# Halving the mixer lane's rate and holding its work behind the main line in a hybrid decoder trunk

## The chip, the cores and the metric

The kernel runs on one core of one Trainium2 chip. The metric is the device time of one execution in microseconds; lower is better. The engines are named as the profile names them: PE is TensorE, DVE is VectorE, ACT is ScalarE, POOL is GpSimd, SP is the queue that issues the loads and stores.

## The reference, cut to what matters

The kernel computes DEPTH = 2 layers over 1024 tokens of width 1024. Each layer is a mixer of three head groups, a channel MLP and a gated embedding:

```python
def hybrid_layer(h, p_i, ...):
    xn = rmsnorm(h, attn_norm_g)
    z = xn @ w_in
    za, zq, zk, zv, zc = jnp.split(z, ...)
    ya = chunk_gmlp(za, ...)
    q = apply_rope(rmsnorm(q, q_norm_g), cos, sin)
    k = apply_rope(rmsnorm(k, k_norm_g), cos, sin)
    yb = swa_sink_attention(q, k, v, sinks)          # window 128
    yc = s5_ssm(zc, ...)
    y = jnp.concatenate([rmsnorm(ya, ...), rmsnorm(yb, ...), rmsnorm(yc, ...)], axis=-1)
    h = h + y @ w_out
    hn = rmsnorm(h, mlp_norm_g)
    h = h + jnp.square(jax.nn.relu(hn @ w_ff1)) @ w_ff2      # D_FF = 4096
    gate = jax.nn.sigmoid(rmsnorm(h, ple_norm_g) @ w_ple_gate)
    return h + gate * (p_i @ w_ple_proj)
```

## The kernel before

**Halves and windows.** The tokens are cut into two halves of 512 (h = 0, 1). The dense part of a layer for one half (the MLP and the gate) is a *window*; there are four, in the order (layer 0, half 0), (0, 1), (1, 0), (1, 1), called windows 0 to 3 here. A window goes through the MLP in 8 chunks: four groups of 24 matmuls (FF1, 128x512 each, with a high and a low part of each operand), then eight groups of 12 (FF2), which add into H. Behind the last chunk comes the *tail*: the sum of squares of H, its rstd, and then the gate with eight groups of 24. That makes 1728 matmuls of the main line in a window.

**The lane.** The mixer of the window after the next one (projection, attention, S5, gMLP, then mix_out with eight groups of 24 matmuls by w_out) is a Python generator, a *lane*. The window's code yields every 12 matmuls, and at each such step `tick` advances the lane by RATE pieces. So the program text itself alternates main line and lane. After that the tile framework's scheduler places the instructions of each engine by its own model of time, and may move a lane instruction ahead of main ones that were traced before it. Each engine then runs its instructions strictly in the resulting order. The left lane (the mixer of half 1 of layer 0) runs at RATEL = 3.0, and is `nxt` for window 0.

**The norm's scale.** `rstd_wide` (from L283) sums over the partitions by one matmul into a PSUM bank, tag "o", which exists once and is shared by every caller with that tag; then VectorE scales it (L289), makes a seed (L293) and goes three rounds (ACT's square L295, VectorE L296 and L297), reading the bank until the last L296. mix_out calls it for the MLP's norm (its output is `rbc`, read by r at L1344), the window's tail for the gate's norm (read by gt at L1390).

**Banks.** Of the eight PSUM banks mm and s have two each, x, p, t and o one. In the MLP `fbank` goes round mm, mm, x; in the gate round mm, s, x, mm, s, p, so the sixth group behind one writes its bank again, which gt of that group (L1390) must have read.

**Weights.** `load_w` loads a 512 KB piece, ACT casts its high part (L104), VectorE subtracts for the low part (L105). The main line's ring has three w buffers, the mixer's has two.

**Around the change.** The first window follows mix_out(0, 0), which `run` drives by itself (`finish`), with the left lane advancing beside it; the left lane's attention prepares k (L1078 to L1117: gt, tab, kt, k, kst), transposes it on PE (pk L1120, kT L1122), and prepares and transposes q (rt, qst L1143 to L1151, pq L1188, qt L1191), then multiplies (pss L1201).

Of the kernel before, what the change touches and what calls it, by code (L numbers as in the profile page):

```python
# [16 lines left out]
P = 128  # L17
# [4 lines left out]
NK = D // P  # L22
# [16 lines left out]
PASSES = ((0, 0), (1, 0), (0, 1))  # L39


RATE, RATE0, RATEL = 3.0, 2.0, 3.0


class Ring:

    def __init__(self, trunk, stg, pool, plan, ahead):
        self.t, self.stg, self.pool, self.plan, self.ahead = trunk, stg, pool, plan, ahead
        self.loaded = []
# [13 lines left out]
class Trunk:  # L63


    def __init__(self, tc, ctx, a):
        self.tc, self.ctx, self.a = tc, ctx, a
        self.nc = nc = tc.nc
        self.V, self.S, self.G, self.T, self.Q = nc.vector, nc.scalar, nc.gpsimd, nc.tensor, nc.sync
        self.lanes, self.nbank, self.nz, self.flags = [], 0, 0, set()  # L70
        self.X, self.R, self.H, self.hst = {}, {}, {}, {}

    def pool(self, stack, name, bufs=1, **kw):
        return stack.enter_context(self.tc.tile_pool(name=name, bufs=bufs, **kw))
# [123 lines left out]
    def finish(self, e):  # L198
        self.until(lambda: e[3])

    def main(self, gen):
        for _ in gen:
            self.tick()

    def wait(self, *flags):
        while not all(f in self.flags for f in flags):
# [1116 lines left out]
    def window(self, l, h, stages):  # L1323

        a, V, S, G, T, Q = self.a, self.V, self.S, self.G, self.T, self.Q
        st, fp = self.stage("ff", h)
        F, H = self.fring, self.H[h]
        last = l == DEPTH - 1
        A = fp.tile([P, 2, 4, HALF], F32R, name="A")
        nch = DFF // 512  # L1330

        def f2(w, m, ps, tail):
            V.tensor_tensor(H[:, m], H[:, m], ps, ALU.add)  # L1333
            if tail is not None:
                self.add_sq(H, m, tail, fp, "r", 2)
                self.split_x(h, m, self.g_ple(l, m))

        for c in range(nch):
            tail = None
            for m in range(4):  # L1340
                w, ps = F.next(), self.fbank()
                self.main(self.cm(ps, w, 0, self.X[h], range(NK)))
                r = fp.tile([P, 512], F32, tag="r", name="r", bufs=2)
                V.scalar_tensor_tensor(r, ps, 0.0, self.R[h][1], ALU.max, ALU.mult)  # L1344
                q = fp.tile([P, 512], F32, tag="r", name="q", bufs=2)
                S.activation(A[:, 0, m], r, AF.Square)  # L1346
                S.activation(q, r, AF.Square)  # L1347
                V.tensor_tensor(A[:, 1, m], q, A.bitcast(F32)[:, 0, m], ALU.subtract)  # L1348
            if c == nch - 1:
                self.until(lambda: stages <= self.flags and ("prep", 1) in self.flags)  # L1350
                pst, pp = self.stage("ple", h)
                pjs = []

                def load_pj():
                    if len(pjs) < NK:
                        t = pp.tile([P, 512], F32, tag="pj", name="pj", bufs=4)
                        Q.dma_start(t, self.pj[l][h][len(pjs)])
                        pjs.append(t)

                for _ in range(4):  # L1360
                    load_pj()
                tail = fp.tile([P, 512], F32, name="nacc")
                self.new_x(h)
            for i in range(4):
                w = F.next()
                if i == 0:

                    pss = [self.fbank() for _ in range(2)]
                    for j in range(2):
                        self.main(self.cm(pss[j], w, j * P, A, (0, 1, 2), stop=False))  # L1370
                    for j in range(2):
                        self.main(self.cm(pss[j], w, j * P, A, (3,), start=False))
                    self.tick()
                    self.tick()
                    for j in range(2):
                        f2(w, j, pss[j], tail)
                    continue
                for j in range(2):
                    ps = self.fbank()
                    self.main(self.cm(ps, w, j * P, A, range(4)))  # L1380
                    f2(w, 2 * i + j, ps, tail)
        self.rstd_wide(tail, D, EPS, h, (fp, "r", 2))
        acc = None
        if not last:
            acc = fp.tile([P, 512], F32, name="nacc")
        for m in range(NK):
            pg = self.fbank(("mm", "s", "x", "mm", "s", "p"))
            self.main(self.cm(pg, F.next(), 0, self.X[h], range(NK)))
            t = fp.tile([P, 512], F32, tag="r", name="gt", bufs=2)
            V.tensor_tensor(t, pg, self.R[h][1], ALU.mult)  # L1390
            S.activation(t, t, AF.Tanh, scale=0.5)
            V.scalar_tensor_tensor(t, t, 1.0, pjs[m], ALU.add, ALU.mult)
            load_pj()
            V.scalar_tensor_tensor(H[:, m], t, 0.5, H[:, m], ALU.mult, ALU.add)
            if not last:
                self.add_sq(H, m, acc, fp, "r", 2)
            else:
                po = self.ps.tile([P, 4, P], F32, tag="to"[m % 2], name="po")
                for b in range(4):
                    T.transpose(po[:, b], H[:, m, b * P:(b + 1) * P], self.ident)  # L1400
                ot = pp.tile([P, 4, P], F32, name="ot", bufs=4)
                S.copy(ot, po)  # L1402
                Q.dma_start(a["out"][0, h * HALF:(h + 1) * HALF, m * P:(m + 1) * P].rearrange("(b p) c -> p b c", p=P),
                            ot)
        if not last:
            Q.dma_start(self.hs[h], H)
            nl = self.lane(self.rstd_lane(acc, D, EPS, h))
            self.step(nl)
            self.new_x(h)
            for k in range(NK):  # L1410
                self.split_x(h, k, self.g_attn(l + 1, k))
        pst.close()
        st.close()
        self.hst[h].close()
        if not last:
            self.finish(nl)
            self.flags.add(("x", l + 1, h))
# [61 lines left out]
    def run(self):  # L1479
        self.setup()  # L1480
        zws, self.zw = ExitStack(), None
        self.zw = self.pool(zws, "zw", 4, side=self.side(0), reuse_waits="tile")
        xs, xp = self.stage("xin", 0)
        left = self.lane(self.left_lane(), RATEL)
        for _ in self.first_x(0, xp, left):
            pass
        x1 = self.lane(self.first_x(1, xp))
        gen = self.project0()
        z0 = self.lane(gen)
        self.until(lambda: x1[3] and ("zq", 0, 0) in self.flags)  # L1490
        xs.close()
        self.until(lambda: {"zg", "rotary"} <= self.flags)
        zws.close()
        self.lanes.remove(z0)
        pzs = ExitStack()
        self.zpools.append(self.pool(pzs, "pz", 2, side=self.side(0), reuse_waits="tile"))
        self.lane(self.gmlp(0, 0, 0, "x", [("attn", 0, 0)]), RATE0)
        self.until(lambda: True)
        self.lane(self.attention(0, 0, 0), RATE0)
        self.main(gen)  # L1500
        self.main(self.embed())
        self.until(lambda: {("attn", 0, 0), ("gm", 0, 0)} <= self.flags)
        self.zpools.pop()
        pzs.close()
        self.finish(self.lane(self.mix_out(0, 0, self.fring, "mm", 3)))
        seq = [(l, h) for l in range(DEPTH) for h in range(2)]
        nxt = left
        for i, (l, h) in enumerate(seq):
            self.window(l, h, self.stages(*seq[i + 1]) if i + 1 < len(seq) else set())
            if i + 1 < len(seq):  # L1510
                self.finish(nxt)
            if i + 2 < len(seq):
                nxt = self.lane(self.mix_lane(*seq[i + 2]), RATE)
# [30 lines left out]
```

## Time and profile before

| | us |
|---|---|
| median of 3 runs (lowest, highest) | 2381.81 (2376.33, 2382.33) |
| the profiled execution, its own time | 2379.47 |
| its span in the trace | 2377.7 |
| PE busy | 2321.7 |
| VectorE busy | 1552.6 |
| ScalarE busy | 1026.9 |

The span is what the trace covers; the execution's own time is 1.8 us longer. PE's busy time is modelled from pipelined matmuls, so a busy share of 98% says that PE seldom waits, not that it runs at its peak. Window 0 begins at about 337 us; the last gt of the gates of windows 0 to 2 starts at 842.36, 1411.99 and 1969.14 us. A timeline row names start, busy time, engine, line and operation, and in square brackets the idle time just before it with what ended it.

### The profile page before, as it was taken

The numbers are of one execution on the slowest core, as the hardware profiler recorded it, in microseconds if no ns is written. First come the engines' busy times: TensorE is split into PE (matmuls) and PEld (weight loads), VectorE is DVE, ScalarE is ACT, GpSimd is POOL, SyncE is SP. The second block draws the span as 40 slices with busy tenths as digits, with TensorE's granted clock in tenths as the row PEclk, the third lists the DMA queues.
The fourth block names the chain that finished last, engine by engine and source line by source line (L and its number), as shares of the span: only waits on it lengthen the run. The fifth ranks groups of instructions, "written<-read, shape, count | busy, mean of one in ns | idle before, by whom it ended". The sixth has DMA issues, their size and how long they took to land. (4 is left out here: it accounts for less than half of the span.)

```text
span 2377.7 us, 29270 instructions
## 1 busy us (share of the span) xinstructions
PE 2321.7 (98%) x10941; PEld 1884.9 (79%) x10941; DVE 1552.6 (65%) x2700; ACT 1026.9 (43%) x1787; POOL 5.4 (0%) x15
## 2 busy tenths in 40 slices
PE   7998899999999999999999999999999999999998
PEld 5887677788788887777888888777888888888887
DVE  7877768675966765675585774676657675444455
ACT  7427646433334443553342543464334443322333
POOL 0000000000000000000000000000000000000000
PEclk9997999999999999999999999999999999999999
DMA  8663632253553335324443344422434425333333
GB/s 244 191 203 120 210 100 61 79 179 101 145 156 99 114 126 146 103 75 139 128 135 120 102 138 132 137 76 80 159 103 141 127 80 150 98 95 94 96 94 101
DMA packets 403558, 295.94 MB, mean 124 GB/s; under 512 B 66668, under 2 KB 376024, under 8 KB 401624
## 3 DMA queue, kind: packets, MB, share of 16 engines
q1 hardware_dynamic: 403416, 294.07, 41.2%
q8 instruction: 86, 1.41, 0.3%
q14 instruction: 56, 0.46, 0.1%
HBM read 250.48 MB, written 43.54 MB: 124 GB/s over the span
## 5 line engine op out<-in xcount | busy, mean ns | idle before, releaser
L104 ACT CAST w<-st 128x1024 fp32r<-128x1024 f32 x364 | 387.8, 1067 | 857.6 <-PE mm_ps L359 435.9
L359 PE MATMUL mm_ps<-x,w 128*128 128x512 f32 x2904 | 704.0, 394 | 8.1 <-ACT x L89 4.2
L359 PEld LDWEIGHTS mm_ps<-x,w 128*128 128x128 f32 x2904 | 542.0, 189 | 132.0 <-issue 10.1
L105 DVE TENSOR_TENSOR w<-st,w 128x1024 fp32r<-128x1024 f32 x364 | 448.6, 1234 | 202.8 <-ACT w L104 201.8
L359 PE MATMUL mm_ps<-A,w 128*128 128x512 f32 x2016 | 500.9, 392 | 2.6 <-DVE H L1333 2.6
L359 PEld LDWEIGHTS mm_ps<-A,w 128*128 128x128 f32 x2016 | 375.9, 188 | 85.3 <-DVE H L1333 5.1
L359 PE MATMUL x_ps<-A,w 128*128 128x512 f32 x1056 | 272.9, 393 | 4.1 <-DVE H L1333 4.1
L359 PE MATMUL x_ps<-x,w 128*128 128x512 f32 x1104 | 272.0, 394 | 0.0
L359 PE MATMUL s_ps<-x,w 128*128 128x512 f32 x1056 | 252.9, 391 | 5.1 <-DVE w L105 2.9
L359 PEld LDWEIGHTS x_ps<-x,w 128*128 128x128 f32 x1104 | 205.7, 188 | 45.4 <-issue 3.4
L359 PEld LDWEIGHTS s_ps<-x,w 128*128 128x128 f32 x1056 | 198.0, 188 | 49.8 <-DVE w L105 4.2
L359 PEld LDWEIGHTS x_ps<-A,w 128*128 128x128 f32 x1056 | 196.7, 188 | 50.8 <-DVE H L1333 8.3
L1333 DVE TENSOR_TENSOR H<-H,mm_ps 128x512 f32<-128x512 f32 x168 | 113.2, 683 | 84.0 <-PE mm_ps L359 83.2
L1344 DVE SCALAR_TENSOR_TENSOR r<-mm_ps,rbc 128x512 f32<-128x512 f32 x88 | 60.7, 689 | 118.2 <-PE mm_ps L359 118.0
L1333 DVE TENSOR_TENSOR H<-H,x_ps 128x512 f32<-128x512 f32 x88 | 60.2, 684 | 68.8 <-PE x_ps L359 68.2
L710 PE MATMUL s_ps<-w,x 128*128 128x512 f32 x384 | 100.3, 401 | 4.4 <-ACT x L89 2.5
L1348 DVE TENSOR_TENSOR A<-q,A 128x512 fp32r<-128x512 f32 x128 | 87.7, 685 | 3.6 <-ACT q L1347 3.5
L710 PEld LDWEIGHTS s_ps<-w,x 128*128 128x128 f32 x384 | 72.9, 193 | 21.3 <-ACT x L89 2.9
L1346 ACT ACTIVATE A<-r 128x512 fp32r<-128x512 f32 x128 | 80.1, 626 | 7.5 <-DVE r L1344 7.4
L1347 ACT ACTIVATE q<-r 128x512 f32<-128x512 f32 x128 | 78.9, 616 | 0.0
L1224 ACT ACTIVATE pr<-pr,anm,hf 128x128 f32<-128x128 f32 x128 | 61.7, 485 | 17.5 <-DVE anm L1221 17.5
L89 ACT ACTIVATE x<-H,gT 128x512 fp32r<-128x512 f32 x80 | 53.7, 711 | 14.1 <-PE s_ps L359 8.3
(386 smaller groups left out, 2114.9 us busy)
## 6 DMA issues: line engine op xcount, KB each, us to landing
st<-in_w_ff SPq DMA_DIRECT2D x256, 512.0 KB, 4.1
st<-in_w_out SPq DMA_DIRECT2D x32, 512.0 KB, 4.1
st<-in_w_ple_gate SPq DMA_DIRECT2D x32, 512.0 KB, 4.1
st<-in_w_in SPq DMA_DIRECT2D x18, 512.0 KB, 4.7
p<-par SPq DMA_DIRECT2D x8, 1024.0 KB, 8.4
pj<-pjz SPq DMA_DIRECT2D x32, 256.0 KB, 2.2
H<-hs SPq DMA_DIRECT2D x4, 2048.0 KB, 7.8
pj<-pj SPq DMA_DIRECT2D x32, 256.0 KB, 3.3
```

The costliest lines, as they stand in the source:

```text
L89: self.S.activation(hi, x, AF.Copy, scale=g)
L104: self.S.copy(hi, src)
L105: self.V.tensor_tensor(lo, src, hi.bitcast(F32), ALU.subtract)
L359: self.T.matmul(ps, w[:, i, k, c0:c0 + P], X[:, j, k, :], start=(start and n == 0), stop=(stop and n == last))
L710: T.matmul(pss[b], X[:, j, 2 * s + kk, c], w[:, i, kk, :], start=(s == 0 and kk == 0 and n == 0), stop=(s == 3 and kk == 1 and n == 2))
L1224: S.activation(pr[:, i], pr[:, i], AF.Exp, bias=nm[:, i:i + 1], scale=f[:, i:i + 1], accum_out=den[:, i:i + 1])
L1333: V.tensor_tensor(H[:, m], H[:, m], ps, ALU.add)
L1344: V.scalar_tensor_tensor(r, ps, 0.0, self.R[h][1], ALU.max, ALU.mult)
L1346: S.activation(A[:, 0, m], r, AF.Square)
L1347: S.activation(q, r, AF.Square)
L1348: V.tensor_tensor(A[:, 1, m], q, A.bitcast(F32)[:, 0, m], ALU.subtract)
```

## The change

RATE goes from 3.0 to 1.5, for the lanes of the mixer and, by `nxt[1] = RATE`, for what is left of the left lane in window 0. And `main(..., True)`, used for nearly all groups of a window, wraps each step of the lanes in `issue_after` of the last instruction of PE, VectorE and ScalarE that the main line had traced since the window's start (`mark`): on these three engines the scheduler may not place what the lanes trace in that step ahead of it. It is a constraint on the order alone.

```diff
-RATE, RATE0, RATEL = 3.0, 2.0, 3.0
+RATE, RATE0, RATEL = 1.5, 2.0, 3.0
+ENGINES = (mybir.EngineType.PE, mybir.EngineType.DVE, mybir.EngineType.Activation)
...
+        self.mark, self.last = 0, {e: None for e in ENGINES}
...
-    def main(self, gen):
+    def main(self, gen, behind=False):
         for _ in gen:
-            self.tick()
+            if not behind:
+                self.tick()
+                continue
+            traced = self.nc.cur_bb.bb.instructions
+            for i in traced[self.mark:]:
+                if i.engine in self.last:
+                    self.last[i.engine] = i
+            with ExitStack() as st:
+                for i in self.last.values():
+                    if i is not None:
+                        st.enter_context(self.tc.issue_after(i))
+                self.tick()
+            self.mark = len(traced)
...
         st, fp = self.stage("ff", h)
+        self.mark = len(self.nc.cur_bb.bb.instructions)
...
-                self.main(self.cm(ps, w, 0, self.X[h], range(NK)))
+                self.main(self.cm(ps, w, 0, self.X[h], range(NK)), True)
...
-                        self.main(self.cm(pss[j], w, j * P, A, (0, 1, 2), stop=False))
+                        self.main(self.cm(pss[j], w, j * P, A, (0, 1, 2), stop=False), True)
...
-                    self.main(self.cm(ps, w, j * P, A, range(4)))
+                    self.main(self.cm(ps, w, j * P, A, range(4)), True)
...
-            self.main(self.cm(pg, F.next(), 0, self.X[h], range(NK)))
+            self.main(self.cm(pg, F.next(), 0, self.X[h], range(NK)), True)
...
         nxt = left
+        nxt[1] = RATE
```

In the rows below, the lines of the changed kernel are 18 or 19 higher than the same ones of before (L359 is L377 there, rstd_wide's L288 to L297 are L306 to L315, L1390 is L1409).

*PE, gate of window 1.* s_ps with x0 is mix_out's (the lane), s_ps, mm_ps, p_ps and x_ps with x1 are gate groups; o_ps_11492 is the matmul of the tail's rstd, o_ps_10776 (o_ps_9995 before) the one of mix_out's. Before:

```order
L359 MATMUL p_ps_11586<-x1_11321,w_11511 128x512 x3
L288 MATMUL o_ps_11492<-nacc_11320,onesr_93 128x512
L359 MATMUL p_ps_11586<-x1_11321,w_11511 128x512 x13
L359 MATMUL mm_ps_11626<-x1_11321,w_11549 128x512
L359 MATMUL s_ps_11666<-x1_11321,w_11589 128x512
L359 MATMUL mm_ps_11626<-x1_11321,w_11549 128x512 x23
L359 MATMUL s_ps_11666<-x1_11321,w_11589 128x512 x23
L359 MATMUL x_ps_11704<-x1_11321,w_11629 128x512 x24
L359 MATMUL mm_ps_11742<-x1_11321,w_11669 128x512 x24
```

And now:

```order
L377 MATMUL s_ps_10726<-x0_8277,w_10648 128x512 x23
L377 MATMUL mm_ps_11508<-x1_11321,w_11408 128x512
L377 MATMUL s_ps_11546<-x1_11321,w_11451 128x512 x24
L377 MATMUL p_ps_11586<-x1_11321,w_11511 128x512 x24
L377 MATMUL mm_ps_11626<-x1_11321,w_11549 128x512 x4
L306 MATMUL o_ps_10776<-nacc_10304,onesr_93 128x512
L377 MATMUL mm_ps_11626<-x1_11321,w_11549 128x512 x20
L377 MATMUL s_ps_11666<-x1_11321,w_11589 128x512 x24
L377 MATMUL x_ps_11704<-x1_11321,w_11629 128x512 x13
L306 MATMUL o_ps_11492<-nacc_11320,onesr_93 128x512
L377 MATMUL x_ps_11704<-x1_11321,w_11629 128x512 x11
L377 MATMUL mm_ps_11742<-x1_11321,w_11669 128x512 x24
```

mix_out's last group has moved from the last chunk of the MLP into the gate's first group, its o_ps stands in the gate, and the tail's o_ps has moved from the third gate group (p_ps) to the fifth (x_ps).

*VectorE, the same place.* o_ps_11492 and rbc_11495 are the tail's rstd, rbc_10779 is mix_out's; w is a weight of the main ring. Now:

```order
L314 SCALAR_TENSOR_TENSOR rs_a_10780<-rs_a_10780,o_ps_10776 128x512
L315 SCALAR_TENSOR_TENSOR rbc_10779<-rs_a_10780,rbc_10779 128x512
L109 TENSOR_TENSOR w_11707<-st_11705,w_11707 128x1024
L307 TENSOR_SCALAR o_ps_11492<-o_ps_11492 128x512
L311 TENSOR_SCALAR rbc_11495<-o_ps_11492 128x512
L314 SCALAR_TENSOR_TENSOR rs_a_11496<-rs_a_11496,o_ps_11492 128x512
L315 SCALAR_TENSOR_TENSOR rbc_11495<-rs_a_11496,rbc_11495 128x512
L109 TENSOR_TENSOR w_11745<-st_11743,w_11745 128x1024
L314 SCALAR_TENSOR_TENSOR rs_a_11496<-rs_a_11496,o_ps_11492 128x512
L315 SCALAR_TENSOR_TENSOR rbc_11495<-rs_a_11496,rbc_11495 128x512
```

The tail's chain stands directly behind mix_out's, with one w in its second round; before, mix_out's chain was done in the MLP's last chunk.

*VectorE, start of window 0.* x0_3389 is the split of H for the MLP, o_ps_3390 the rstd that r waits for; hf, tab, rt, kt, k and kst belong to the left lane's attention. Before:

```order
L90 SCALAR_TENSOR_TENSOR x0_3389<-H0_3113,gT_107,x0_3389 128x512 x7
L105 TENSOR_TENSOR w_3428<-st_3426,w_3428 128x1024
L1117 TENSOR_TENSOR kst_3528<-k_3447,kst_3528 128x2x64
L329 TENSOR_TENSOR nacc_3118<-nacc_3118,nsq_3386 128x512
L90 SCALAR_TENSOR_TENSOR x0_3389<-H0_3113,gT_107,x0_3389 128x512
L289 TENSOR_SCALAR o_ps_3390<-o_ps_3390 128x512
```

And now:

```order
L109 TENSOR_TENSOR w_3428<-st_3426,w_3428 128x1024
L1096 TENSOR_SCALAR gt_3453<-gt_3453 128x64
...
L1121 TENSOR_TENSOR k_3447<-k_3447,hf_109 128x640
L347 TENSOR_TENSOR nacc_3118<-nacc_3118,nsq_3386 128x512
L94 SCALAR_TENSOR_TENSOR x0_3389<-H0_3113,gT_107,x0_3389 128x512
...
L1161 TENSOR_TENSOR rt1_3498<-q_3479,tab0_3458 128x512
L1125 TENSOR_TENSOR kt2_3482<-k_3447,tab1_3464 128x10x32 x2
L1127 TENSOR_TENSOR k_3447<-k_3447,tab1_3464 128x640
L1128 TENSOR_TENSOR k_3447<-k_3447,kt2_3482 128x640
L307 TENSOR_SCALAR o_ps_3390<-o_ps_3390 128x512
```

The preparation of k, which stood in mix_out(0, 0), has moved between the splits of x and the first step of the rstd.

## Rows read from the trace of the kernel before

**Rows 1.** The page, busy time and share of each engine.

```profile
PE 2321.7 (98%) x10941; PEld 1884.9 (79%) x10941; DVE 1552.6 (65%) x2700; ACT 1026.9 (43%) x1787; POOL 5.4 (0%) x15
```

**Rows 2.** Stretches of 100 us: length, busy time (count) of each engine, clock, DMA.

```profile
1300.00:1400.00 100.00, 99.67 (x436) 81.58 (x435) 73.30 (x100) 47.70 (x69) 0.00 (x0) 1.00 0.39 111
...
2100.00:2200.00 100.00, 99.34 (x438) 81.66 (x437) 44.85 (x53) 28.42 (x36) 0.00 (x0) 1.00 0.33 98
```

**Rows 3.** Timeline of PE, start of window 0.

```profile
357.05 0.66 PE L1188 MATMUL pq<-identr,qst 128*128 128x128 f32 x4 [1.78 <-ACT kT L1122]
...
361.52 2.08 PE L1201 MATMUL pss<-kT,qt 128*128 128x256 f32 x8 [0.73 <-ACT qt L1191]
363.39 4.92 PE L359 MATMUL mm_ps<-x,w 128*128 128x512 f32 x16
```

**Rows 4.** Timeline of VectorE, start of window 0.

```profile
336.14 0.69 DVE L1310 TENSOR_TENSOR H<-H,mm_ps 128x512 f32<-128x512 f32 x1 [2.53 <-PE mm_ps L359]
...
341.55 1.22 DVE L105 TENSOR_TENSOR w<-st,w 128x1024 fp32r<-128x1024 f32 x1
...
348.87 0.70 DVE L289 TENSOR_SCALAR o_ps<-o_ps 128x512 f32<-128x512 f32 x1 [4.57 <-PE o_ps L288]
...
361.66 0.68 DVE L1344 SCALAR_TENSOR_TENSOR r<-mm_ps,rbc 128x512 f32<-128x512 f32 x1
```

**Rows 5.** Timeline of VectorE in mix_out(0, 0), the left lane's preparation of k.

```profile
297.15 0.83 DVE L1103 TENSOR_TENSOR k<-k,hf 128x640 f32<-128x640 f32 x1 [2.25 <-DMA k<-zg]
...
299.44 0.20 DVE L1078 TENSOR_SCALAR gt<-gt 128x64 f32<-128x64 f32 x1 [0.67 <-DMA gt<-in_q_norm_g]
...
304.69 0.69 DVE L1144 TENSOR_TENSOR rt<-q,tab 128x512 f32<-128x512 f32 x1
```

**Rows 6.** Stretches of 5 us, columns as in rows 2.

```profile
360.00:365.00 5.00, 4.27 (x17) 3.79 (x16) 5.00 (x12) 3.21 (x9) 0.00 (x0) 0.50 0.13 47
365.00:370.00 5.00, 5.00 (x24) 4.12 (x24) 5.00 (x15) 3.71 (x13) 0.00 (x0) 0.93 0.17 52
960.00:965.00 5.00, 2.75 (x15) 2.06 (x14) 2.39 (x4) 3.08 (x6) 0.00 (x0) 1.00 0.27 93
```

**Rows 7.** Timeline of PE in mix_out(0, 0), around groups of pk.

```profile
319.13 0.56 PE L1120 MATMUL pk<-identr,kst 128*128 128x128 f32 x4
319.53 10.69 PE L359 MATMUL mm_ps<-x,w 128*128 128x512 f32 x46
...
336.92 0.73 PE L359 MATMUL mm_ps<-x,w 128*128 128x512 f32 x2 [0.42 <-ACT x L89]
```

**Rows 8.** Timeline of PE, gate of window 2.

```profile
1941.47 1.02 PE L288 MATMUL o_ps<-nacc,onesr 128*128 128x512 f32 x2
1941.93 2.16 PE L359 MATMUL x_ps<-x,w 128*128 128x512 f32 x7
```

**Rows 9.** Timeline of VectorE, gate of window 2.

```profile
1942.53 0.70 DVE L289 TENSOR_SCALAR o_ps<-o_ps 128x512 f32<-128x512 f32 x1 [0.93 <-PE o_ps L288]
...
1947.07 0.69 DVE L297 SCALAR_TENSOR_TENSOR rbc<-rs_a,rbc 128x512 f32<-128x512 f32 x1
...
1949.18 0.69 DVE L297 SCALAR_TENSOR_TENSOR rbc<-rs_a,rbc 128x512 f32<-128x512 f32 x1
...
1953.06 0.69 DVE L1390 TENSOR_TENSOR gt<-p_ps,rbc 128x512 f32<-128x512 f32 x1
```

**Rows 10.** Timeline of PE, rows with a wait: windows 0 to 2.

```profile
595.79 3.01 PE L359 MATMUL x_ps<-A,w 128*128 128x512 f32 x12 [1.15 <-DVE H L1333]
...
932.69 5.55 PE L359 MATMUL s_ps<-x,w 128*128 128x512 f32 x23 [1.43 <-DVE w L105]
...
964.09 0.66 PE L1120 MATMUL pk<-identr,kst 128*128 128x128 f32 x4 [2.25 <-DVE kst L1117]
...
1528.94 0.66 PE L1120 MATMUL pk<-identr,kst 128*128 128x128 f32 x4 [1.15 <-DVE kst L1117]
...
1717.53 4.84 PE L359 MATMUL mm_ps<-A,w 128*128 128x512 f32 x20 [1.34 <-DVE H L1333]
```

## Prediction, made before the changed kernel was run

> **What bounds the kernel now.** I read the engines' line of the page first, then the stretches of 100 us, then PE's timeline with its waits, then the queues behind each wait. PE is busy for 98% of the span [rows 1], so nothing but PE's own time and PE's waits counts, and the chain of waits is no help: it stays on PE almost to the end. In a stretch of the last window, where no lane runs, PE starts 438 matmuls in 100 us, 0.228 us each; in a stretch where the lane's mix_out alternates with the window's matmuls it starts 436 [rows 2]. So a lane that is well fed costs PE its own matmuls and next to nothing for the alternation. What is left to win or lose is where PE waits. The reader is to see two kinds in before. In window 0's start PE waits 1.78 and 0.73 us around the few small matmuls of the lane's attention, which are all the cover there is [rows 3]. Elsewhere the waits are single ones of one or two microseconds [rows 10].
>
> **The change part by part.** It adds and removes no work: on PE, DVE, ACT and SP the instructions are the same ones in another order, and an edge that only orders issue is no wait on the chip. The cost is all in what stands next to what. The load issues on SP move with their steps; PE's covers below are counted from the new order with the loads where they stand now, and no term hangs on them.
>
> *Gates of windows 1 and 2.* This is the largest term. At half the rate the lane comes to mix_out later, and its 192 matmuls now end in the gate's first group. mix_out's rstd and the tail's rstd share the one PSUM bank "o", mix_out's comes first, and so the tail's o_ps matmul stands deep in the fifth gate group, with 11 matmuls of that group behind it (order of PE, window 1; window 2 reads alike with s_ps for x_ps and p_ps for mm_ps). The sixth group writes the bank of the first, which gt has to read, and gt needs the tail's rstd. No lane matmul is left as a cover: mix_out was its last piece. Count from the start of that o_ps on PE. PE's side: o_ps itself 0.46 (1941.47 to the next matmul at 1941.93) and 11 matmuls of 0.228 make 3.0 us [rows 2, 8]. DVE's side by window 2 of before: its first step starts 1.06 us after PE's (1941.47 to 1942.53), the first round's last step 4.54 later (1947.07), a clean round takes 2.11 (1947.07 to 1949.18), so two more make 4.22, and from the last rbc to gt's end go 0.73 and 0.69: 11.2 us [rows 8, 9]. The first round there had a w of the ring in it (1.2 on DVE, as at 341.55 [rows 4], and its cast on ACT ahead of it), which made it about 1.7 longer than the seed's 0.73 and a round of 2.11; with no w at all the chain is 9.5 us. The new order has one w in the second round. So PE waits between 9.5 - 3.0 = 6.5 and 11.2 - 3.0 = 8.2 us; I take 7.3. The upper bound is the chain that window 2 really had, 12.3 us from o_ps to gt's end at 1953.75 with its two w, less 3.0: 9.3. A gain is excluded here, since before has 85 matmuls (13 + 1 + 1 + 23 + 23 + 24, its order for window 1), 19 us, between the two, and so no wait. Twice 7.3 is **+14.6**.
>
> *The clock behind these two waits.* In window 0's bubble the granted clock was 0.50 (the 1.2 GHz level) over 360 to 365 and 0.93 over 365 to 370, so it came back at about 365.7; the main line had resumed at 363.39, and 2.3 us at half speed lose 1.2 us [rows 3, 6]. The single wait of 2.25 us at 962 left the clock at 1.00 [rows 6, 10]. A wait of 7 us is nearer to the bubble: 1.2 us each, **+2.4**, with 0 and twice that as ends. The Trainium skill (TensorE: Matmul & The Clock Gate, Part 1, The HAM clock gate) has an idle PE fall to 1.2 GHz and come back after sustained work, and names PE's pauses between PSUM banks as one cause (A second HAM failure mode: psum-queue depth-cycling). By that rule alone the short wait at 962 might have cost speed as well, and it didn't; without any clock cost the sum would be 2.4 us lower.
>
> *Start of window 0.* Before had the left lane's key preparation, and three groups of 4 pk matmuls, inside mix_out(0,0), and the other two in the bubble. The mark at the window's start and the edges hold all of it behind the first w load that the window traces. Gained in mix_out: 0.40 us of PE for each of three groups (319.13 to 319.53) and the wait of 0.42 at 336.92, together 1.6 us, so the last H of mix_out is at 334.5 instead of 336.14 [rows 4, 7]. Lost behind it: DVE is through with the first x at 5.4 us behind that H (341.55), as before; then come w (1.14 to the next instruction), hf (0.8), nacc and the last x (1.3), and the gt, tab, rt, kt and k operations (299.44 to 304.69, 5.25), before o_ps: 14.0 us behind H, where before took 12.7 (336.14 to 348.87) [rows 4, 5]. From there to r before took 12.8 [rows 4]. Now three w (3.4), four rt (2.4), qst (0.6) and kst (0.2 each) stand in the chain; the first two rounds have no pause left, and their operations alone, at 0.6 for 512 wide, make 10.1 up to the second round's L314; from there a dependent tail of 4.1 (0.7 + 0.7, ACT's step and DVE's 1.4, 0.7 + 0.7) leads to r: 14.2 us. So r starts at 334.5 + 14.0 + 14.2 = 362.7, and PE's 73rd main matmul 0.9 behind it at 363.6, against 363.39. Meanwhile before had done on PE what is still to do now: 16 pss (2.08 us for eight at half clock, so 2.1 for 16 at full), 8 pq (1.0) and 4 pk (0.2) [rows 3]: 3.3 us. Together 0.2 + 3.3 = **+3.5**. Ends: 0, if the bubble takes no more than now, and 8, if DVE's extra operations come late from ACT and DMA as well.
>
> *Waits that go.* The lane's pk in windows 1 and 2 waited 2.25 and 1.15 us for kst behind a late w_out cast on ACT; the new order puts more than 18 main matmuls, 4 us, between these groups, and the cast isn't ahead of them. At 595.79 PE waited 1.15 for H, behind two x splits of yc (queued on DVE) that now fall into FF1; at 1717.53 it waited 1.34 for H behind a gelu step whose input came late from DMA, where 66 matmuls and more, 15 us, now lie between. I take all four away: 2.25 + 1.15 + 1.15 + 1.34 = **-5.9** [rows 10]. At the least none goes (a wait moves to the next late load); at the most the wait of 1.43 for a w of the projection goes as well, and the like one in window 2 (1.43 too), another -2.9. The order leaves these where they were, so I count them as staying.
>
> Sum on the profiled execution: 2379.5 + 14.6 + 2.4 + 3.5 - 5.9 = 2394.1. The median of the runs lies 2.3 above that execution (2381.81 against 2379.47): **2396 us**.
>
> **The rivals.**
> (a) *Slower still.* The gate's chains keep before's full length, 9.3 us of wait each, window 0 takes 8, half of the savings come: 18.6 + 2.4 + 8 - 3 = +26, so 2408 with the median's 2.3. For it: every tail chain of before has two or three w inside. Against it: the new order has one.
> (b) *No change.* Window 0 costs nothing, the gate's waits stay at 6.5 each with no clock loss, and all waits of the lane go, the projection's too: 13 - 5.9 - 2.9 = +4, so 2386. For it: DVE has pauses of about 0.7 in each clean round (two operations of 0.7 in 2.11 us) of a chain that can take the small operations. That the change does nothing at all is excluded by the order.
> (c) *Faster.* The mechanism is that the main line's waits are the lane's doing: with lane work never ahead, the waits of [rows 10] go (8.8) and window 0's bubble closes (1.78 + 0.73 of waits and 1.2 of clock, 3.7), and the chain of the tail, free of lane work too, gets through behind mix_out's: -12.5, so 2369. It decides at the gates: below 2.7 us for each wait with its clock the kernel is faster beyond what can be told. For it: the lane's operations do stand ahead of H, r and kst in each of those rows. Against it: a chain of three rounds of 2.11 us can't go in the 3.0 us that PE has left, and nothing shortens it; only more matmuls ahead of the full bank would.
> Still another end, that alternation itself slows PE and goes, is spoken against by 436 against 438.
>
> **How the numbers follow.** Forecast (2389 to 2403): 0.50; (a) 0.15; (b) 0.21; (c) 0.14. Differences under 0.3%, about 7 us, can't be told from no change, so no change is 2375 to 2389. From (c) faster 0.14, from (b) same 0.21, the rest slower 0.65. The range has to leave out no more than 2 in 10: from 2379, in the lower half of (b), to 2410, the end of (a).
>
> **What would show it.** Gates: in windows 1 and 2, near the fifth gate group, one wait of PE of 6.5 to 9.3 us ended by DVE's gt, with DVE's L307 to L315 twice in a row ahead of it, and a granted clock under 1 just behind. Window 0: key preparation between x and L307 on DVE, all pk in one stretch after the 72nd main matmul, r at about 364. The pk, yc and gelu waits gone, and stretches outside these places at 228 ns a matmul. I am wrong if the tail's o_ps comes with many matmuls behind it in its group of banks, if a wait at the gates lasts under 2.7 us, or if single waits of some microseconds have appeared in the projection or the attention, where I count none.

## The result, and the profile after

The changed kernel takes 2390.79 us, median of 5 runs (2389.59 to 2394.44), against 2377.89 us (5 runs) for the kernel before: a ratio of 1.0057 (95% interval 1.0046 to 1.0068), so it is slower by about 13 us. The profiled execution, on which the rows below stand, took 2394.44 us with a span of 2392.7, 15.0 more than before's span; it is the longest of its five.

The page's first part of the changed kernel has the same work in a longer span; PE's share went from 98% to 97% [rows 1]:

```profile
PE 2324.1 (97%) x10941; PEld 1887.1 (79%) x10941; DVE 1557.0 (65%) x2700; ACT 1029.0 (43%) x1787; POOL 5.4 (0%) x15
```

PE's timeline at the gate of window 1, and the one wait in the gate of window 2 (to be laid beside [rows 8]):

```profile
1375.04 1.02 PE L306 MATMUL o_ps<-nacc,onesr 128*128 128x512 f32 x2
...
1385.89 3.12 PE L377 MATMUL x_ps<-x,w 128*128 128x512 f32 x13
1388.84 1.02 PE L306 MATMUL o_ps<-nacc,onesr 128*128 128x512 f32 x2
1389.30 3.07 PE L377 MATMUL x_ps<-x,w 128*128 128x512 f32 x11
1399.05 7.62 PE L377 MATMUL mm_ps<-x,w 128*128 128x512 f32 x24 [6.69 <-DVE gt L1409]
...
1967.10 8.52 PE L377 MATMUL p_ps<-x,w 128*128 128x512 f32 x24 [6.68 <-DVE gt L1409]
```

Two o_ps stand 13.8 us apart, mix_out's and the tail's. Behind the second run the 11 matmuls that were left of its group, and then PE waits 6.69 us for gt; the same in window 2. (Counted from one, x_ps is the sixth of the gate's eight groups and the group that waits is the seventh, which writes the bank of the first; ahead of the run they were called the fifth and the sixth. The 11 matmuls between are the same.) The 24 matmuls behind each wait take 7.62 and 8.52 us, where 24 at full speed take 5.60: the wait also costs 2.0 and 2.9 us of clock. VectorE at the same place (beside [rows 9]):

```profile
1383.31 0.68 DVE L314 SCALAR_TENSOR_TENSOR rs_a<-rs_a,o_ps 128x512 f32<-128x512 f32 x1
1384.02 0.69 DVE L315 SCALAR_TENSOR_TENSOR rbc<-rs_a,rbc 128x512 f32<-128x512 f32 x1
1387.21 1.23 DVE L109 TENSOR_TENSOR w<-st,w 128x1024 fp32r<-128x1024 f32 x1 [2.50 <-ACT w L108]
1389.90 0.70 DVE L307 TENSOR_SCALAR o_ps<-o_ps 128x512 f32<-128x512 f32 x1 [1.46 <-PE o_ps L306]
...
1393.53 1.22 DVE L109 TENSOR_TENSOR w<-st,w 128x1024 fp32r<-128x1024 f32 x1
1394.67 0.68 DVE L314 SCALAR_TENSOR_TENSOR rs_a<-rs_a,o_ps 128x512 f32<-128x512 f32 x1
...
1398.22 0.69 DVE L1409 TENSOR_TENSOR gt<-mm_ps,rbc 128x512 f32<-128x512 f32 x1
```

From the tail's o_ps (1388.84) to gt's end (1398.91) go 10.1 us; VectorE was idle 2.50 and 1.46 us just ahead of the chain, so it is not VectorE that came late but the matmul that starts it. Nor did that matmul wait for the bank on the chip: mix_out's last read of it (L314) was over at 1383.99, 4.9 us earlier, and PE was busy all that while. It came late because it stands late in PE's order, which the scheduler fixed with the one bank in its account. The stretches of 5 us around the two waits show the granted clock in the column ahead of the last two:

```profile
1395.00:1400.00 5.00, 0.95 (x2) 0.84 (x3) 4.10 (x7) 1.69 (x3) 0.00 (x0) 0.62 0.37 105
1400.00:1405.00 5.00, 5.00 (x17) 3.95 (x16) 4.86 (x9) 2.04 (x4) 0.00 (x0) 0.70 0.35 105
1405.00:1410.00 5.00, 5.00 (x24) 4.13 (x23) 4.90 (x7) 3.59 (x5) 0.00 (x0) 1.00 0.34 105
...
1960.00:1965.00 5.00, 0.42 (x2) 0.00 (x0) 4.07 (x6) 2.33 (x4) 0.00 (x0) 0.78 0.14 35
1965.00:1970.00 5.00, 2.90 (x7) 2.35 (x8) 4.83 (x8) 1.23 (x2) 0.00 (x0) 0.50 0.33 92
1970.00:1975.00 5.00, 5.00 (x17) 3.94 (x16) 4.90 (x9) 1.65 (x3) 0.00 (x0) 0.69 0.53 187
```

PE's timeline at the start of window 0 (beside [rows 3]):

```profile
352.51 0.56 PE L1138 MATMUL pk<-identr,kst 128*128 128x128 f32 x4
355.87 1.11 PE L1138 MATMUL pk<-identr,kst 128*128 128x128 f32 x4 [2.80 <-DVE kst L1135]
359.85 1.12 PE L1138 MATMUL pk<-identr,kst 128*128 128x128 f32 x4 [2.86 <-DVE kst L1135]
362.16 1.11 PE L1138 MATMUL pk<-identr,kst 128*128 128x128 f32 x4 [1.20 <-DVE kst L1135]
363.49 7.32 PE L377 MATMUL mm_ps<-x,w 128*128 128x512 f32 x20 [0.21 <-DVE r L1363]
```

And the three rows of VectorE on which the hand sum for this place rested (beside [rows 4]):

```profile
334.41 0.69 DVE L1328 TENSOR_TENSOR H<-H,mm_ps 128x512 f32<-128x512 f32 x1 [2.53 <-PE mm_ps L377]
...
348.85 0.70 DVE L307 TENSOR_SCALAR o_ps<-o_ps 128x512 f32<-128x512 f32 x1 [0.78 <-PE o_ps L306]
...
362.74 0.69 DVE L1363 SCALAR_TENSOR_TENSOR r<-mm_ps,rbc 128x512 f32<-128x512 f32 x1
```

The main line resumes at 363.49, as good as at the time of before (363.39), but with only 16 pk done in the bubble, and it stays slow longer: 20 matmuls take 7.32 us, where 20 at full speed take 4.70. The last thing to see is where waits have gone. Behind the bubble, in windows 0 to 2, before had waits over 0.4 us of 10.9 us in all (the five of [rows 10], and four of 0.96, 0.49, 1.43 and 0.68 in the projections); in their places the changed kernel has three, in the projections of windows 1 and 2:

```profile
945.77 0.50 PE L377 MATMUL s_ps<-x,w 128*128 128x512 f32 x1 [0.97 <-ACT w L108]
...
1508.79 5.51 PE L377 MATMUL s_ps<-x,w 128*128 128x512 f32 x23 [1.42 <-DVE w L109]
1515.48 0.47 PE L377 MATMUL s_ps<-x,w 128*128 128x512 f32 x1 [1.17 <-DVE rs_a L87]
```

Two new ones stand in window 0, which the late lane work may explain (e4 below):

```profile
640.38 2.33 PE L377 MATMUL mm_ps<-A,w 128*128 128x512 f32 x9 [0.52 <-DVE r L1363]
646.81 3.04 PE L377 MATMUL x_ps<-A,w 128*128 128x512 f32 x12 [0.89 <-DVE H L1352]
```

### The profile page after: what moved, and what is told of

Its sections match the earlier page's. It is cut to its first block, busy times and chain, and to the rows that moved or that the text cites. A ratio compares the mean times of both kernels' runs of the same rounds, so it can differ in the third digit from the quotient of the medians.

```text
span 2392.7 us, 29253 instructions
## 1 busy us (share of the span) xinstructions
PE 2324.1 (97%) x10941; PEld 1887.1 (79%) x10941; DVE 1557.0 (65%) x2700; ACT 1029.0 (43%) x1787; POOL 5.4 (0%) x15
## 5 line engine op out<-in xcount | busy, mean ns | idle before, releaser
L377 PE MATMUL mm_ps<-x,w 128*128 128x512 f32 x2904 | 703.0, 395 | 14.6 <-ACT x L93 7.7
L377 PEld LDWEIGHTS mm_ps<-x,w 128*128 128x128 f32 x2904 | 544.5, 189 | 135.2 <-issue 12.7
L377 PE MATMUL mm_ps<-A,w 128*128 128x512 f32 x2016 | 501.5, 392 | 2.1 <-DVE H L1352 1.6
L377 PEld LDWEIGHTS mm_ps<-A,w 128*128 128x128 f32 x2016 | 375.9, 188 | 88.1 <-issue 5.5
L377 PE MATMUL x_ps<-A,w 128*128 128x512 f32 x1056 | 275.1, 394 | 3.6 <-DVE H L1352 3.5
L377 PE MATMUL x_ps<-x,w 128*128 128x512 f32 x1104 | 270.9, 393 | 0.0
L377 PE MATMUL s_ps<-x,w 128*128 128x512 f32 x1056 | 252.3, 391 | 3.7 <-DVE w L109 1.4
L377 PEld LDWEIGHTS x_ps<-x,w 128*128 128x128 f32 x1104 | 205.9, 188 | 45.2 <-issue 3.1
L377 PEld LDWEIGHTS x_ps<-A,w 128*128 128x128 f32 x1056 | 196.3, 188 | 50.7 <-DVE H L1352 7.7
L377 PEld LDWEIGHTS s_ps<-x,w 128*128 128x128 f32 x1056 | 198.1, 188 | 48.1 <-ACT w L108 3.3
L1365 ACT ACTIVATE A<-r 128x512 fp32r<-128x512 f32 x128 | 80.3, 628 | 15.2 <-DVE r L1363 14.4
```

What stands on the lines that cost most here:

```text
L377: self.T.matmul(ps, w[:, i, k, c0:c0 + P], X[:, j, k, :], start=(start and n == 0), stop=(stop and n == last))
```

## The experiments

Each run stands beside runs of the kernel before on the same chip; times are medians, and 0.1% is 2.4 us. A difference of two ratios is good to about 4 us. A finer measure comes from the traces. In mix_out(0, 0) PE waits for the last part of x (3.78 us in before, until 293.24). In each kernel 1339 matmuls stand ahead of this point and 9602 behind it, but PE goes on from it anywhere from 289.55 to 296.04 us, with and without the change. Counted from there to the end of the span, what varies ahead of it drops out:

```profile
293.24:2377.73 2084.49, 2058.15 (x9602) 1674.31 (x9602) 1331.83 (x2094) 854.34 (x1404) 2.86 (x3) 1.00 0.39 115
292.41:2392.70 2100.29, 2062.84 (x9602) 1678.24 (x9602) 1338.74 (x2096) 858.27 (x1406) 2.87 (x3) 0.99 0.38 114
291.75:2363.91 2072.16, 2053.44 (x9602) 1674.41 (x9602) 1332.57 (x2094) 854.82 (x1404) 2.87 (x3) 1.00 0.39 116
```

These are before, the changed kernel and e5 (columns as in [rows 2]). Little is lost by starting there: in the changed kernel the wait for x is 6.93 us, but three waits ahead of it (1.22, 1.43 and 0.94 in before) are gone, so that the sum is 6.9 against 7.4. For all of them, one execution each:

| | PE goes on in mix_out(0, 0) | from there to the end | against before |
|---|---|---|---|
| before | 293.24 | 2084.5 | |
| e6: before, bank t | 289.55 | 2084.7 | +0.2 |
| changed | 292.41 | 2100.3 | +15.8 |
| e8: changed again | 292.35 | 2098.8 | +14.3 |
| e1: changed, bank t | 291.70 | 2080.7 | -3.8 |
| e4: changed, window 0 free | 291.39 | 2090.1 | +5.7 |
| e5: changed, both repairs | 291.75 | 2072.2 | -12.3 |
| e2: ordering at the old rate | 292.48 | 2084.6 | +0.1 |
| e3: rate alone | 291.02 | 2084.7 | +0.2 |
| e7: rate alone, bank t | 292.09 | 2079.9 | -4.6 |
| e9: ordering alone, both repairs | 292.49 | 2080.7 | -3.8 |
| e10: both, ordering on PE alone, both repairs | 296.04 | 2077.1 | -7.4 |

The two executions of the changed kernel differ by 1.5 us in this measure, so differences under about 2 us say nothing. The theory from the prediction and the rows: the lower rate brings mix_out into the gate, where its rstd holds PSUM bank "o" and keeps the tail's matmul back (two waits and their clock); the ordering makes the bubble of window 0 worse; and against that stand the waits that went. The rival for the first: two chains of rstd are in each other's way on VectorE and ScalarE, whatever the bank.

**e1: the tail's rstd in another bank.**

```diff
-        self.rstd_wide(tail, D, EPS, h, (fp, "r", 2))
+        self.rstd_wide(tail, D, EPS, h, (fp, "r", 2), "t")
```

> The changed kernel with one word more: the tail's rstd_wide takes PSUM bank t instead of o, so that it needn't wait for mix_out's rstd. In the order the tail's matmul now stands in the gate's first group, with over 90 matmuls ahead of the sixth group. Theory (the shared bank makes the two waits of 6.7 us and the half-clock stretches of about 2.1 and 2.9 us behind them): all 18 us go, 2391 - 18 = 2373, below the kernel before. Rival (the two chains stand in each other's way on VectorE whatever the bank): most of each wait stays, at least 4 us each, and the time is 2383 or more. Rival (the wait only moves to the next window's r, since mix_out's rstd now comes second): two waits of some microseconds at the starts of windows 2 and 3.

Measured: 2375.47 us, ratio 0.9991 (0.9981 to 1.0). The waits at both gates are gone. PE's timeline of e1 where the first one was:

```profile
1373.77 1.98 PE L377 MATMUL mm_ps<-x,w 128*128 128x512 f32 x8
1375.59 1.02 PE L306 MATMUL o_ps<-nacc,onesr 128*128 128x512 f32 x2
1376.05 4.20 PE L377 MATMUL mm_ps<-x,w 128*128 128x512 f32 x16
1380.09 5.60 PE L377 MATMUL s_ps<-x,w 128*128 128x512 f32 x24
1385.53 5.60 PE L377 MATMUL x_ps<-x,w 128*128 128x512 f32 x24
1390.97 5.60 PE L377 MATMUL mm_ps<-x,w 128*128 128x512 f32 x24
```

The only o_ps here is mix_out's; the group that waited before (1390.97) follows without a pause, and every 24 matmuls take 5.60 us. On VectorE the two chains now lie 38 us apart, and gt of the first group has long been read:

```profile
1339.05 0.70 DVE L307 TENSOR_SCALAR t_ps<-t_ps 128x512 f32<-128x512 f32 x1 [0.41 <-PE t_ps L306]
1363.24 0.68 DVE L1409 TENSOR_TENSOR gt<-mm_ps,rbc 128x512 f32<-128x512 f32 x1
...
1377.40 0.69 DVE L307 TENSOR_SCALAR o_ps<-o_ps 128x512 f32<-128x512 f32 x1
```

So the shared bank it was, by way of the order: one word moves the tail's matmul from the sixth gate group into the first. The rival isn't excluded by this run alone, since it parts the two chains on VectorE as well; against it stands the trace of the changed kernel, in which VectorE was idle just ahead of the tail's chain and that chain, once started, took 10.1 us, where 9.5 to 11.2 had been counted for it alone. Nor did the wait move to the next windows. The gain is 16 us by the ratios, 1.0058 (e8 below) to 0.9991, and 18 to 20 by the table, where 18 were expected.

**e2: the ordering with the old rate.**

```diff
-RATE, RATE0, RATEL = 1.5, 2.0, 3.0
+RATE, RATE0, RATEL = 3.0, 2.0, 3.0
```

> The changed kernel with RATE back at 3.0, so only the ordering behind the main line is left. In the order mix_out's rstd of window 1 is done in the MLP's last chunk again, and the tails' matmuls have 60 to 80 matmuls behind them, while the start of window 0 reads as in the changed kernel. Theory (the rate makes the gate's waits, the ordering makes the longer bubble of window 0): no wait at the gates, window 0's bubble as in the changed kernel (4 to 5 us more than before), some single waits gone: 2378 + 4 - 4, so 2376 to 2382. Rival (the ordering itself makes the loss, by late lane work everywhere): about 2390.

Measured: 2378.79 us, ratio 1.0 (0.9991 to 1.0009). As expected: no wait at a gate, the pk waits of the bubble as in the changed kernel (3.00, 2.85, 1.20, and 1.08 for r). So the rate is what brings the gates' waits, and the ordering is what makes the bubble longer.

**e3: the rate without the ordering.**

```diff
-RATE, RATE0, RATEL = 3.0, 2.0, 3.0
+RATE, RATE0, RATEL = 1.5, 2.0, 3.0
...
         nxt = left
+        nxt[1] = RATE
```

> The kernel before with RATE 1.5 and nxt[1] = RATE, without the ordering. In the order the start of window 0 reads as in before; in window 1's gate the tail's matmul has 49 matmuls behind it before the full bank, in window 2's gate 11 as in the changed kernel. Theory: one wait of 6.7 us with its clock (2.9) in window 2, none or under 1 us in window 1, no longer bubble in window 0, and the pk waits gone: 2378 + 9.6 + 0.5 - 3 = 2385. Rival (the ordering is needed for the loss): 2378 or less.

Measured: 2378.54 us, ratio 1.0006 (0.9998 to 1.0015). By the time alone the rival would have been right (2378 or less); the trace decides. The wait is where the order had it, in window 2 alone, and of the size of the changed kernel's (6.68):

```profile
1940.62 1.02 PE L288 MATMUL o_ps<-nacc,onesr 128*128 128x512 f32 x2
1941.07 3.07 PE L359 MATMUL s_ps<-x,w 128*128 128x512 f32 x11
1950.83 7.62 PE L359 MATMUL p_ps<-x,w 128*128 128x512 f32 x24 [6.69 <-DVE gt L1390]
```

But the time is 6 us lower than expected: the lower rate alone takes more waits away than I gave it. Of those over 0.4 us behind the bubble, the gate's aside, 4.8 us are left, where before had 10.9. The place of the expectation held, its savings were too small. So the rate alone brings the wait in one of the two gates; in window 1 it takes the ordering as well.

**e4: window 0 without the ordering.** The changed kernel with `self.first = (l, h) == (0, 0)` in `window`, and in `main`:

```diff
-            if not behind:
+            if not behind or self.first:
```

> The changed kernel, but in window 0 the lane's work may be issued ahead as before (rate and the other windows as changed). In the order the pk groups stand inside mix_out(0, 0) again. Theory: window 0's bubble is back at before's size, 4 to 5 us shorter, and the gates' waits stay: 2391 - 4.5 = 2386.5. Rival (what window 0 loses comes later in the window, from the lower rate): 2390 or more.

Measured: 2384.64 us, ratio 1.003 (1.0019 to 1.0041), against 1.0058 for the changed kernel: 6.7 us. The same step from e1 to e5 is 9.5 us by the ratios, and by the table both are larger than expected, 8.6 to 10.1 and 8.6. PE's timeline of e4 at the end of the bubble, and one of its gates:

```profile
359.87 2.08 PE L1219 MATMUL pss<-kT,qt 128*128 128x256 f32 x8 [0.73 <-ACT qt L1209]
361.75 6.85 PE L377 MATMUL mm_ps<-x,w 128*128 128x512 f32 x24
...
1389.07 8.59 PE L377 MATMUL mm_ps<-x,w 128*128 128x512 f32 x24 [6.69 <-DVE gt L1410]
```

The pq and pss are back in the bubble, and the 24 matmuls behind it lose 1.25 us to the clock (6.85 against 5.60); the 20 of the changed kernel lost 2.6 (7.32 against 4.70). The waits at 640 and 646 are gone as well, and of the three in the projections one of 1.13 us is left. The gates' waits stay.

**e8: the changed kernel again**, as the base for the repairs.

> The changed kernel once more, beside the others on the same chip, as the base that the repairs are counted from: 2390 to 2392, with the two waits of 6.7 us at the gates and the longer bubble in window 0.

Measured: 2392.3 us, ratio 1.0058 (1.0045 to 1.0071), with waits of 6.69 and 6.69 us at the gates. Of the two waits in window 0 it has the one of 0.89 alone, at 646.42.

**e5: both repairs**, the edits of e1 and e4 together.

> The changed kernel with both repairs: the tail's rstd in bank t, and window 0's lane free to be issued ahead. Theory (the two losses are separate places and add): the changed kernel's time less 15 to 18 for the gates and less 4 to 6 for window 0, so about 2369, below the kernel before by some 8 us, which is what the waits that went are worth. Rival (the losses overlap, one repair moves work into the other place): no lower than the better of the two single repairs, 2375.

Measured: 2367.3 us, ratio 0.9951 (0.9938 to 0.9964): faster than both kernels, by 25 and by 12 us. The two losses are separate. PE in the stretch in which before was at its worst behind window 0's start, with four waits over 0.4 us, in before and in e5:

```profile
900.00:1000.00 100.00, 94.33 (x436) 76.65 (x435) 57.78 (x100) 42.49 (x77) 0.00 (x0) 1.00 0.45 128
900.00:1000.00 100.00, 99.78 (x462) 82.95 (x461) 57.23 (x95) 37.97 (x64) 0.00 (x0) 1.00 0.47 132
```

**e6: bank t in the kernel before**, the edit of e1.

> The kernel before with the tail's rstd in bank t. In the order of before 49 matmuls and more stand behind each tail's matmul, and no gate has a wait. Theory (bank o costs nothing as long as mix_out's rstd is done ahead of the gate): the same time as before, within 2 us. Rival (the shared bank costs something in any order, so that the repair of the changed kernel is no evidence on the change): 3 us and more below before.

Measured: 2378.66 us, ratio 0.9998 (0.9988 to 1.0007). The shared bank costs nothing in the old order, in which mix_out's rstd is over before the gate.

**e7: rate and bank t, no ordering**, the edits of e3 and e1.

> The kernel before with RATE 1.5 and bank t, without the ordering. Theory (the lower rate itself takes the waits for pk, H and the projection away, and its one gate wait of 6.69 us with its half-clock stretch of about 2.5 goes with the bank): 2378.5 - 9 = 2369.5, the same as the changed kernel with both repairs, so that the ordering is worth nothing. Rival (the ordering itself takes waits away): 2 us and more slower than the kernel with both repairs.

Measured: 2374.08 us, ratio 0.9983 (0.9975 to 0.9992). The rival holds: without the ordering it is 7 us slower than e5. Its trace keeps waits for w, for the statistics of z and for pk, in the projection, the gate and the attention, that e5 doesn't have:

```profile
931.38 5.53 PE L359 MATMUL s_ps<-x,w 128*128 128x512 f32 x23 [1.13 <-DVE w L105]
937.50 0.47 PE L359 MATMUL s_ps<-x,w 128*128 128x512 f32 x1 [0.59 <-DVE rs_a L84]
...
1358.57 3.94 PE L359 MATMUL s_ps<-x,w 128*128 128x512 f32 x16 [0.76 <-DVE w L105]
...
1528.73 0.66 PE L1120 MATMUL pk<-identr,kst 128*128 128x128 f32 x4 [0.99 <-DVE kst L1117]
```

**e9: e5 with the old rate**, the ordering with both repairs.

```diff
-RATE, RATE0, RATEL = 1.5, 2.0, 3.0
+RATE, RATE0, RATEL = 3.0, 2.0, 3.0
```

> The kernel with both repairs (bank t, window 0 free), but RATE back at 3.0: the ordering without the rate. With the rate alone (ratio 0.998) and both (0.995) it completes a square. Theory (rate and ordering take different waits away and add): before is 2379, rate alone saved about 5, both 12, so the ordering alone saves 7: 2372. Rival (the ordering only pays where the rate leaves main matmuls between the lane's): 2377 to 2379, no different from before.

Measured: 2374.93 us, ratio 0.9988 (0.9977 to 0.9999). Between theory and rival: 3 us, not 7. With the losses repaired the rate alone is worth 4 us (interval 2 to 6), the ordering alone 3 (0.2 to 5.5), both together 12 (9 to 15). So they seem to help each other; the medians alone would hardly show it, but the table has 4.6 and 3.8 against 12.3. In e9 the wait at 595 (1.15), one for pk (1.06) and one of 1.42 for w are still there. My reading, which no run shows, is that the ordering needs main matmuls between the lane's pieces to put the lane behind, and that at the old rate there are too few.

**e10: e5 with the ordering on PE alone.**

```diff
-ENGINES = (mybir.EngineType.PE, mybir.EngineType.DVE, mybir.EngineType.Activation)
+ENGINES = (mybir.EngineType.PE,)
```

> The kernel with both repairs and RATE 1.5, but the ordering put on PE alone (with VectorE and ScalarE alone the order of every engine comes out the same as with all three, so that this one needs no run). Theory (the waits that the ordering takes away are those for H, r and w behind the lane's work on VectorE and ScalarE): as the lower rate with bank t and no ordering, 2374 to 2375. Rival (PE's own order does it): 2367 to 2369, as with all three.

Measured: 2374.84 us, ratio 0.9987 (0.9978 to 0.9996), by the medians the same as e7, as the theory had it. The table shows a little more: e7 is 4.6 below before, e10 7.4 and e5 12.3. So most of what the ordering is worth comes with VectorE and ScalarE; some 3 us of it may come with PE, which the medians can't tell from nothing.

## Why the prediction was right, point by point

The forecast was slower, 2396 us in a range of 2379 to 2410; the measured median is 2390.8. The sign, the places and the mechanism hold. But three of the four terms were mis-sized: the clock and window 0 cost 8.2 us more than forecast, and the waits that went saved 6.4 us more. That these nearly cancel is luck.

*The gates* (+14.6 predicted, 7.3 a wait). Measured 6.69 and 6.68, in windows 1 and 2, behind the matmul and ahead of the group that the order showed, ended by gt: 13.4. The chain took 10.1 us from o_ps to gt's end, between the 9.5 and 11.2 of the hand sum. The one w in its second round cost 0.5 us of the chain (that round took 2.64 us, the third 2.11), since it fell into the pause that each round has for ScalarE's step. e1 shows that the shared bank is the cause, e3 that the rate alone brings the wait of window 2, e6 that the bank costs nothing in the old order.

*The clock behind them* (+2.4, at the most 4.8). Mis-sized: 2.0 and 2.9 us, together 4.9 in this execution. I sized it by the bubble of before, in which small matmuls ran between the waits and the speed came back 2.3 us behind the main line's return. Here PE stood still for 6.7 us. By the stretches the granted clock fell 3.9 us into the wait in window 1 and 2.4 us in window 2, and full speed came back some 4 us after the return in window 1, 6 us in window 2. Only the price by the row of the bubble was wrong, not the mechanism.

*The start of window 0* (+3.5). Mis-sized, and by the most. The hand sum's times came out almost exactly: H at 334.41 (334.5 predicted), r at 362.74 (362.7), the main line's return at 363.49 (363.6). That is partly luck, since PE went on in mix_out(0, 0) 0.8 us earlier in this execution than in that of before (292.41 against 293.24). Counted from there, H came 0.9 us earlier and not 1.6: of the three groups of pk one stood at 335.94, behind the last matmul that H needs, and the wait of 0.42 for x didn't go but is 0.81 now. And the main line came back 0.9 us later, not 0.2, with pss, pq and pk of 3.1 us still to do. Two things were missing: the clock, which behind longer idle stretches cost 2.6 us instead of 1.2 (I had taken it as equal), and the left lane's late work, which e4 shows to bring two waits of 0.52 and 0.89 us at 640 and 647. 0.9 + 3.1 + 1.4 + 1.4 = 6.8. In the projections of windows 1 and 2, e4 also has 2.4 us less of waits: 0.97 + 1.42 + 1.17 against 1.13. Together 9.2, where e4 gives 6.7 by the ratios and 8.6 to 10.1 by the table.

*The waits that go* (-5.9, at the most -8.8). All four went, as predicted. Mis-sized: e5, which has the savings without the losses, is 12 us below before. In e5 the three waits of window 1's projection went as well (0.96, 1.43 and 0.49); the 1.43 I had counted as staying, the other two I had left out. All waits over 0.4 us behind the bubble came down from 10.9 us to 3.3 in e5. That accounts for 7.6 of the 12. The rest isn't in shorter pauses: from that point in mix_out(0, 0) on, PE's idle time of every length fell from 26.3 to 18.7 us, the same 7.6. The other 4.7 are in PE's busy time for the same 9602 matmuls, 2058.2 us in before and 2053.4 in e5, and I have not taken that apart.

So in sum 13.4 + 4.9 + 9.2 - 12.3 = +15.2, where the spans of the two profiled executions differ by 15.0, the medians by 12.9 and the prediction's sum was +14.6. The terms were off by -1.2 at the gates, +2.5 in the clock, +5.7 in window 0 and -6.4 in the savings. That 2396 lies 5 us above the median comes for the larger part from the 2.3 us that were added for the median of before: that was a median of three executions, and with five it lies 1.6 us below the profiled one, not 2.3 above.

Rival (a) failed at the gates, where the waits were 6.7 us and not 9.3, though its 8 us for window 0 was nearer than my 3.5. Rival (b) failed on the clock and on window 0. Rival (c), that the main line's waits are the lane's doing, was half right. Its price, -12.5, is what e5 measured, but by luck: 3.7 of it was the bubble's closing, and the bubble of e5 still has waits of 2.35, 0.68 and 0.73 us. What kept the changed kernel from it is the two places, and its claim that the tail's chain gets through behind mix_out's is what failed. Had the tail's rstd stood in another bank, the same change would have been level with before (e1), and with window 0 left free as well faster by 0.5% (e5).

## What to carry to other kernels

Slowing a background lane moves its last stage to a later place, and the question is what that place shares with the foreground: here one PSUM bank that both use for a few microseconds put a matmul late in the order, which made a wait of 6.7 us twice, and a different bank name took it away. Count in the instruction order how many matmuls stand between the start of a serial chain and the first instruction that needs its result: 11 matmuls, 2.5 us, against a chain of 10 was all that was needed to see it ahead of the run. When a tuned change comes out slower, price its good part apart from its bad one: here a net loss of 13 us hid a gain of 12. And where the start of a program varies from one execution to the next, count from a point behind it: before and e6 agree to 0.2 us in that count, where their starts differ by 3.7.

## What the runs showed of the hardware that was not expected

The half-clock stretch behind a wait differed with the same wait: 24 matmuls behind 6.69 us of idle PE took 7.62, 8.52, 8.10, 7.54, 8.59 and 8.46 us in the gates of three executions (the changed kernel's two and e4's), against 5.60 at full speed, so a loss of 1.9 to 3.0 us. A price from one row is good to about 1 us here. That the loss varies agrees with the Trainium skill (TensorE: Matmul & The Clock Gate, Part 1, The HAM clock gate), which has the gate look at the engine on a schedule of its own.
